# Turning the second memory's score matrices with VectorE and DRAM instead of TensorE

## The chip, the cores and the metric

The kernel runs on one core of a Trainium2 chip. The metric is the device time of one execution in microseconds (us). The kernel before took 2047.61 us, the median of three runs (2044.39, 2047.61 and 2047.65). All profile numbers come from one further execution that the hardware profiler recorded.

## The reference, cut to what matters

The reference is one encoder layer, applied to two independent sequences of 512 tokens by 1024 channels (here called sequence 0 and sequence 1). Each passes through a half-step SwiGLU feed-forward, a mixing block, a second half-step feed-forward and a final RMS norm. The mixing block projects the normed input once and runs two branches side by side: grouped-query attention with 8 heads, and an mLSTM matrix memory with 4 heads of 128 channels that reads in both directions. Each branch is projected back to 1024 channels, gated, summed, and sent through one output projection.

For one memory head the kernel computes, without the reference's chunks,

```
scores[t, s]  = q[t] . k[s] / sqrt(128)                       512 x 512
T[t, s]       = scores * (forward decay weights)  / (forward divisor of t)     for s <= t
              + scores * (backward decay weights) / (backward divisor of t)    for s >= t
h[:, t]       = sum over s of  v[s, :] * T[t, s]                128 x 512
out[:, t]     = sigmoid(o) * head_norm * h[:, t] / rms(h[:, t])
```

T comes out with the query token t on the partitions. The product with v needs the key token s on the partitions, so T has to be turned, once per head and sequence: 512 x 512 float32 values.

## The kernel before, in words

Almost all the work is matmuls on TensorE (PE), each value split into a high and a low part and each product made of three matmuls of 128x128 by 128x512. The feed-forwards stand before and after the mixing; the change touches only the mixing of sequence 1.

`mix(s, ...)` (L841) writes the mixing of sequence s. The weight-bound projections are **units**, pairs of a load and a computation. `go` (L771) issues a unit's weight load, holds the unit, and writes the computation of the oldest held unit once more than `ahead` units are held; for sequence 1 `ahead` is 2 (L844). `queue` and `fill(n)` (L847) feed units to `go`. In sequence 1 all the input projection's weights come back, already split, from DRAM, two DMAs of 512 KB a unit on SyncE's (SP's) queue (L293) into a pool `w8` of 4 buffers. Units used here:

- `mem_values` (L998): four units of 48 matmuls, the values v of all heads;
- `mem_qk(h, j)` (L1009): q or k of head h, 24 matmuls; sequence 1 keeps each result in a tile of the pool `wr` (4 buffers of 4 KB a partition);
- `att_gate`, `out_gate`, `mem_gate(d)`: gates, 24 matmuls each; `mem_gate` keeps its result in a tile of the pool `t2` (11 buffers) until `merge_mem(d)`;
- `merge_att(d)`, `merge_mem(d)`: the branches' projections back, 12 matmuls each.

`mem_head(h)` (L1231) writes a head's scores (12 matmuls, L1241, into two PSUM banks of the pool `ps`), the decay weights on ScalarE (L1255), their product on VectorE (L1257), and the normalisation (L1268 to L1271). It leaves four tiles `Ts[i][0]` of 128x512, one for each block of 128 query tokens.

`mem_out(h, Ts)` (L1274) turns and uses them. For each key block j, four TensorE transposes of 128x128 against the identity (L1283) fill a PSUM bank of the pool `pt`; ScalarE and VectorE split it into high and low parts (`split`, L715 and L716); three matmuls with v (L1291) add it to the bank `po`. Then come the squares, the column sums through VectorE's 32x32 transpose (L225) and a small matmul (L232), the reciprocal root, its spreading (L258), and the split into `mem` (L1302, L715, L716), which `merge_mem` reads.

The order of the instructions on each engine is made by a planner: it takes instructions by priority, which is the order of writing unless `shifted` moves it, and by when its own cost model holds them ready. `pin` (`keep_in_program_order`) ties an instruction to the written order among the pinned instructions of its engine. In the attention part nearly every matmul is pinned; in the memory part of the kernel before none is. The head loop (L1305) writes `mem_head(h)`, some units, `mem_out(h)`, and the rest of the queue, for h = 0 to 3; after it come the eight `mem_gate` and the eight `merge_mem`.

Of the kernel before, what the change touches and what calls it, by code (L numbers as in the profile page):

```python
# [8 lines left out]
F32 = mybir.dt.float32  # L9
F32R = mybir.dt.float32r  # L10
I32 = mybir.dt.int32
AF = mybir.ActivationFunctionType
# [4 lines left out]
P = 128  # L17
S = 512
D = 1024
KD = D // P  # L20
# [6 lines left out]
def encoder(ctx, tc, I, outs):  # L27
    nc = tc.nc
    cpool = ctx.enter_context(tc.tile_pool(name="cpool", bufs=1))
    dpool = ctx.enter_context(tc.tile_pool(name="dpool", bufs=1, space=bass.MemoryType.DRAM))  # L30
    apool = ctx.enter_context(tc.tile_pool(name="apool", bufs=7))
    wpool = ctx.enter_context(tc.tile_pool(name="wpool", bufs=3))
# [9 lines left out]
    def nm(s):  # L42
        n_id[0] += 1
        return f"{s}_{n_id[0]}"
# [241 lines left out]
    def load_w(view, key, park=True):  # L286


        if key in parked:
            d, shape = parked[key]  # L290
            w2 = wpool.tile(shape, F32R, tag="w8", bufs=4, name=nm("w"))
            for i in range(2):
                nc.sync.dma_start(f(w2[:, i]), d[:, i])  # L293
            return w2[:, 0], w2[:, 1]
        raw = fetch_w(view)
        with shifted(-WEIGHTS):
            hi, lo = split_w(raw, V_)
        if not park:
            return hi, lo
        shape = [P, 2] + list(raw.shape[1:])  # L300
        parked[key] = d, _ = dpool.tile(shape, F32, name=nm("wpark")), shape
        for i, t in enumerate((hi, lo)):
            nc.sync.dma_start(d[:, i], f(t))
        return hi, lo
# [3 lines left out]
    V_ = nc.vector  # L308
# [404 lines left out]
    def split(src, hi, lo, eng=None):  # L713

        nc.scalar.activation(hi, src, AF.Copy)  # L715
        (eng or V_).tensor_tensor(lo, src, f(hi), op=ALU.subtract)  # L716
# [3 lines left out]
    HM, DM = 4, 128  # L720
# [46 lines left out]

    held = []
    ahead = [1]

    def go(*units):  # L771
        for load, comp in units:
            held.append((comp, load()))
            while len(held) > ahead[0]:
                c, w = held.pop(0)
                c(w)
# [6 lines left out]
    def tok_proj(xh, xl, cols, kk, done, banks):  # L783

        N = sum(n for _, n in cols)
        p = []

        def load(k0):
            return load_w([win_v[:, k0:k0 + kk, c:c + n] for c, n in cols], ("in", cols[0], k0))

        def comp(k0, w):
            wh, wl = w
            if not p:
                p.extend(b() for b in banks)
            for kl in range(kk):
                k = k0 + kl
                for b in range(4):
                    bs = slice(b * P, (b + 1) * P)
                    for i, (a, w_) in enumerate(((xh, wh), (xh, wl), (xl, wh))):
                        nc.tensor.matmul(p[b][:, :N], a[:, k, bs], w_[:, kl, :],  # L800
                                         start=(k == 0 and i == 0), stop=(k == KD - 1 and i == 2))
# [26 lines left out]
    def proj_w(wh, wl, src, n, p=None):  # L828
        p = p or MM()
        for k in range(n):  # L830
            sh, sl = src(k)
            for i, (a, b) in enumerate(((wh, sh), (wh, sl), (wl, sh))):
                nc.tensor.matmul(p, a[:, k, :], b, start=(k == 0 and i == 0), stop=(k == n - 1 and i == 2))  # L833
        return p

    OUT = 3
    FILLER = 5,3
    SOON = 7,1
    FIRST = 7,9,9,11

    def mix(s, xh, xl, early=None, extra=None, after=None):  # L841

# [8 lines left out]
        def F2(dtype=F32):  # L851
            return T2(dtype, "f2")
# [156 lines left out]
        def mem_qk(h, j):  # L1009
            def done(pp):  # L1010
                if j == 0 and not s:
                    t = wpool.tile([P, 4, S], F32R, tag="w8", bufs=4, name=nm("qk"))
                    qks[h] = [t[:, i] for i in range(4)]
                elif s:
                    t = wpool.tile([P, 2, S], F32R, tag="wr", bufs=4, name=nm("qk"))
                    qks.setdefault(h, []).extend(t[:, i] for i in range(2))
                t = pp
                if not s:
                    t = F2()
                    V_.tensor_tensor(t, pp, R[s], op=ALU.mult)  # L1020
# [135 lines left out]
        for b in range(4):  # L1156
            Ps.append(score(0, b))
            next(rope, None)
            among(FIRST[b])
        last = None  # L1160
        for h in range(HA):
            nxt = []
            for b in range(4):
# [16 lines left out]
                last = h, b, pp  # L1180
# [48 lines left out]
        mem = A([P, HM, 2, S], F32R, "mem")  # L1229

        def mem_head(h):  # L1231
# [39 lines left out]
                    V_.tensor_scalar(tf[:, up_], tb[:, up_], rb, None, op0=ALU.mult)  # L1271
            return Ts

        def mem_out(h, Ts):  # L1274
            vm = Vm[0]
            po = PO()
            hs_ = slice(h * P, (h + 1) * P)
            turned = []
            for j in range(4 + 1):
                if j < 4:  # L1280
                    p = PT()
                    for i in range(4):
                        nc.tensor.transpose(p[:, i * P:(i + 1) * P], Ts[i][0][:, j * P:(j + 1) * P], ident)  # L1283
                    ph, pl = T2(F32R), T2(F32R)
                    split(p, ph, pl)
                    turned.append((j, ph, pl))
                if j >= 1:
                    t, ph, pl = turned.pop(0)
                    with shifted(15):
                        for n, (a, b) in enumerate(((0, ph), (1, ph), (0, pl))):  # L1290
                            nc.tensor.matmul(po, vm[:, a, t, hs_], b, start=(t == 0 and n == 0),  # L1291
                                             stop=(t == 3 and n == 2))
            h2 = T2()
            nc.scalar.activation(h2, po, AF.Square)
            og = ogs[h]
# [9 lines left out]
        for h in range(HM):  # L1305
# [12 lines left out]
            fill(99)  # L1318

        mh, ml = A([P, KD, S], F32R, "mh"), A([P, KD, S], F32R, "ml")  # L1320
        go(*[mem_gate(d) for d in range(KD)])
        go(*[merge_mem(d) for d in range(KD)])
        flush()
        yield None
# [20 lines left out]
    pin = tc.keep_in_program_order  # L1345

    def busy(n, idle):

        for _ in range(n):
# [3 lines left out]
    x2buf = [dpool.tile([P, KD, S], F32, name=f"x2buf{s}") for s in range(2)]  # L1353
    rbuf = [[[dpool.tile([P, 2, S], F32, name=f"rbuf{n}_{j}_{m}") for m in range(7)] for j in range(NF // 2)]
            for n in range(2)]
    xnbuf = dpool.tile([P, KD, S], F32, name="xnbuf")
    raws = [A([P, 4, D], F32, "raw")]
    x0r_ = A([P, KD, S], F32, "x0r")
# [288 lines left out]
    r = [None, None]  # L1647
# [213 lines left out]
```

## Time and profile before

| what | value |
|---|---|
| median of three runs | 2047.61 us (2044.39 to 2047.65) |
| the profiled execution: its own time | 2046.24 us |
| the profiled execution: span from first to last instruction | 2044.5 us |
| TensorE busy | 2034.3 us, 9313 matmuls and transposes |
| VectorE busy | 1571.5 us |
| ScalarE busy | 909.1 us |
| GpSimd busy | 93.6 us |
| granted TensorE clock | 0.999 |
| memory part of sequence 1 in the span, scores of head 0 to output of head 3 | 1180.75 to 1287.4 us |

In the rows below an engine is PE (TensorE matmul), PEld (its weight load), DVE (VectorE), ACT (ScalarE), POOL (GpSimd) or SP (SyncE); a "q" behind it means its sequencer, which issues DMAs. L and a number is a line of the kernel. `out<-in` gives the tiles, `x12` a count. A matmul's record runs to its modelled end, and the next one starts before that, so the distance between two starts, and not the length of a record, is what a matmul costs.

### The profile page before, as it was taken

The numbers are of one execution on the slowest core, as the hardware profiler recorded it, in microseconds if no ns is written. First come the engines' busy times: TensorE is split into PE (matmuls) and PEld (weight loads), VectorE is DVE, ScalarE is ACT, GpSimd is POOL, SyncE is SP. The second block draws the span as 40 slices with busy tenths as digits, with TensorE's granted clock in tenths as the row PEclk, the third lists the DMA queues.
The fourth block names the chain that finished last, engine by engine and source line by source line (L and its number), as shares of the span: only waits on it lengthen the run. The fifth ranks groups of instructions, "written<-read, shape, count | busy, mean of one in ns | idle before, by whom it ended". The sixth has DMA issues, their size and how long they took to land.

```text
span 2044.5 us, 26753 instructions
## 1 busy us (share of the span) xinstructions
PE 2034.3 (100%) x9313; PEld 1680.7 (82%) x9313; DVE 1571.5 (77%) x2780; ACT 909.1 (44%) x1655; POOL 93.6 (5%) x116
## 2 busy tenths in 40 slices
PE   9999999999999999999999999999999999999998
PEld 7888888888888888888888888888888888888887
DVE  7988888886797798786567756366788988786797
ACT  7644444443234577563325554144444444442224
POOL 0000000001003000100120000001000000000001
PEclk9999999999999999999999999999999999999999
DMA  9656566799766853868564345667655655699753
GB/s 308 199 172 224 172 213 187 236 338 362 270 215 223 293 173 130 284 211 292 188 195 139 114 152 169 226 202 225 192 190 181 207 170 180 203 347 341 275 198 119
DMA packets 314727, 445.38 MB, mean 218 GB/s; under 512 B 19848, under 2 KB 189920, under 8 KB 313312
## 3 DMA queue, kind: packets, MB, share of 16 engines
q1 hardware_dynamic: 312512, 437.69, 63.8%
q0 software_dynamic: 1920, 5.72, 0.9%
q8 instruction: 73, 1.20, 0.2%
q14 instruction: 62, 0.51, 0.1%
q10 hardware_dynamic: 160, 0.27, 0.0%
HBM read 284.06 MB, written 159.55 MB: 217 GB/s over the span
## 4 chain that ended last, share of the span: by engine, by line
PE 96%; DVE 2%; ACT 1%; DMA 1%; issue 0%; SPq 0%; DVEq 0%; ACTq 0%
PE mm L833 15%; PE pst L374 12%; PE pso L374 12%; PE mm L374 10%; PE mm L632 8%; PE pss L374 6%; PE mm L820 5%; PE pst L632 4%; PE pss L632 4%; PE mm L800 4%; PE pso L632 3%; PE pso L1121 1%; PE pss L1094 1%; PE pst L1110 1%; PE pso L1291 1%; PE pss L1241 1%
## 5 line engine op out<-in xcount | busy, mean ns | idle before, releaser
L374 PE MATMUL pst<-xc,w 128*128 128x512 f32 x1056 | 253.7, 389 | 0.0
L374 PEld LDWEIGHTS pst<-xc,w 128*128 128x128 f32 x1056 | 198.2, 188 | 41.2
L374 PE MATMUL mm<-xc,w 128*128 128x512 f32 x972 | 229.7, 390 | 0.4 <-ACT f L382 0.4
L374 PEld LDWEIGHTS mm<-xc,w 128*128 128x128 f32 x972 | 182.0, 188 | 38.4 <-ACT f L382 0.8
L632 PE MATMUL mm<-rt,w 128*128 128x512 f32 x765 | 178.7, 389 | 0.0
L833 PE MATMUL mm<-xh,w 128*128 128x512 f32 x560 | 176.9, 392 | 0.0
L632 PEld LDWEIGHTS mm<-rt,w 128*128 128x128 f32 x765 | 143.5, 188 | 29.8
L332 ACT ACTIVATE w<-t 128x512 fp32r<-128x512 f32 x176 | 106.6, 627 | 135.6 <-issue 63.1
L333 DVE TENSOR_TENSOR w<-t,w 128x512 fp32r<-128x512 f32 x176 | 117.8, 687 | 42.9 <-ACT w L332 41.2
L374 PE MATMUL pss<-xc,w 128*128 128x512 f32 x528 | 126.8, 389 | 0.0
L374 PE MATMUL pso<-xc,w 128*128 128x512 f32 x528 | 126.8, 389 | 0.0
L374 PE MATMUL pso<-xc,f 128*128 128x512 f32 x528 | 126.8, 389 | 0.0
L833 PEld LDWEIGHTS mm<-xh,w 128*128 128x128 f32 x560 | 104.9, 188 | 21.9
L374 PEld LDWEIGHTS pss<-xc,w 128*128 128x128 f32 x528 | 99.1, 188 | 20.6
L374 PEld LDWEIGHTS pso<-xc,w 128*128 128x128 f32 x528 | 99.1, 188 | 20.6
L374 PEld LDWEIGHTS pso<-xc,f 128*128 128x128 f32 x528 | 99.1, 188 | 20.6
L820 PE MATMUL mm<-xh,w 128*128 128x512 f32 x336 | 113.4, 400 | 0.0
L833 PE MATMUL mm<-xl,w 128*128 128x512 f32 x280 | 109.6, 391 | 0.0
L715 ACT ACTIVATE w<-wr 128x512 fp32r<-128x512 f32 x72 | 45.1, 632 | 136.7 <-PE pso L632 71.2
L278 ACT ACTIVATE w<-wr 128x1024 fp32r<-128x1024 f32 (+1 forms) x64 | 65.3, 1029 | 79.1 <-issue 23.7
L279 DVE TENSOR_TENSOR w<-wr,w 128x1024 fp32r<-128x1024 f32 (+1 forms) x64 | 79.7, 1247 | 26.5 <-ACT w L278 15.7
L715 ACT ACTIVATE w<-t 128x512 fp32r<-128x512 f32 x82 | 51.8, 632 | 107.6 <-PE pst L632 62.5
(444 smaller groups left out, 4068.7 us busy)
## 6 DMA issues: line engine op xcount, KB each, us to landing
rt<-rbuf SPq DMA_DIRECT2D x154, 512.0 KB, 5.5
wpark<-w SPq DMA_DIRECT2D x88, 512.0 KB, 3.8
w<-wpark SPq DMA_DIRECT2D x88, 512.0 KB, 4.4
wr<-in_ffn_w_gate_dram SPq DMA_DIRECT2D x62, 512.0 KB, 5.3
rbuf<-tab SPq DMA_DIRECT2D x102, 256.0 KB, 4.0
wr<-in_ffn_w_up_dram SPq DMA_DIRECT2D x44, 512.0 KB, 4.5
rbuf<-f SPq DMA_DIRECT2D x72, 256.0 KB, 4.0
wr<-in_w_in_dram SPq DMA_DIRECT2D x36, 512.0 KB, 5.7
```

What stands on the lines that cost most here:

```text
L278: pin(nc.scalar.activation(hi, raw, AF.Copy))
L279: pin(lo_eng.tensor_tensor(lo, raw, f(hi), op=ALU.subtract))
L332: pin(nc.scalar.activation(t[:, 0], src, AF.Copy))
L333: pin(V_.tensor_tensor(t[:, 1], src, f(t[:, 0]), op=ALU.subtract))
L374: nc.tensor.matmul(p, a[:, k, :], xt[:, b, k, :], start=(first and k == 0 and i == 0), stop=(k == HK_ - 1 and i == 2), skip_group_check=True)
L632: nc.tensor.matmul(p, u[:, a, d * P:(d + 1) * P], r[:, b, ts], start=(first and q == 0 and k == 0), stop=(q == len(us) - 1 and k == 2), sk ...
L715: nc.scalar.activation(hi, src, AF.Copy)
L800: nc.tensor.matmul(p[b][:, :N], a[:, k, bs], w_[:, kl, :], start=(k == 0 and i == 0), stop=(k == KD - 1 and i == 2))
L820: pin(nc.tensor.matmul(p[0], a[:, k, :], b, start=(k == 0 and i == 0), stop=(k == n - 1 and i == 2)))
L833: nc.tensor.matmul(p, a[:, k, :], b, start=(k == 0 and i == 0), stop=(k == n - 1 and i == 2))
L1094: pin(nc.tensor.matmul(p, qT[:, h, b * P:(b + 1) * P], kv[:, hk * 2 + j, :], start=(j == 0), stop=(j == 1)))
L1110: pin(nc.tensor.transpose(p[:, b * P:(b + 1) * P], Ps[b][:, kb * P:(kb + 1) * P], ident))
```

## The change

For sequence 1 only:

- `mem_blocks(h, Ts)` is new. VectorE transposes each half row block (128x256) of the four T tiles in 32x32 blocks into two tiles of the pool `wr`: eight instructions a head. Eight DMAs on SP's queue, of 32 partitions each in runs of 512 bytes, put the blocks where they belong in a DRAM buffer; there are two such buffers of 1 MB, used by turns.
- `mem_out` then reads each key block back as a 128x512 tile of the pool `f2` (four DMAs of 256 KB a head, on GpSimd's queue), and splits it from SBUF. No TensorE transposes are left there. The query columns come back in the order (block within 128, block of 128, column), so the output bank `po` has its columns in that order, too; one ScalarE copy a head puts them back into a tile of `t2`, which the squares and the gate read in place of PSUM.
- The head loop is replaced by one written order of heads, units and outputs. `mem_out(h)` is written after `mem_head(h + 1)` and several units. Six `mem_gate` units (`EARLY`) are loaded, and four of them computed, ahead of `mem_out(3)`.
- While this stretch is written, the last matmul of each unit and every matmul of `mem_out` with v is pinned; the score matmuls of `mem_head` aren't.
- q and k of head 2 lie in the tile `mem`, in the places of heads 2 and 3, instead of in `wr`.

The number of units and of their matmuls stays. The core of the diff:

```diff
+    marks = [False]
+    def mark(i, last):
+        return pin(i) if last and marks[0] else i
...
+    EARLY = 6
...
-                    t = wpool.tile([P, 2, S], F32R, tag="wr", bufs=4, name=nm("qk"))
+                    t = mem[:, 2 + j] if h == 2 else wpool.tile([P, 2, S], F32R, tag="wr", bufs=4, name=nm("qk"))
...
+        def mem_blocks(h, Ts):
+
+            q = [wpool.tile([P, 8, 4, 32], F32, tag="wr", bufs=4, name=nm("qt")) for _ in range(2)]
+            for i in range(4):
+                for g in range(2):
+                    V_.transpose(q[g][:, :, i, :],
+                                 Ts[i][0][:, g * 256:(g + 1) * 256].rearrange("p (n m) -> p n m", m=32))
+            for g in range(2):
+                for a in range(4):
+                    nc.sync.dma_start(tbuf[h % 2][8 * g:8 * g + 8, :, a, :].rearrange("n r x -> r n x"),
+                                      q[g][32 * a:32 * a + 32].rearrange("r n i m -> r n (i m)"))
+            return h % 2
...
-                if j < 4:
+                if j < 4 and moved:
+                    p = F2()
+                    nc.gpsimd.dma_start(p, tbuf[Ts][4 * j:4 * j + 4].rearrange("c r a x -> (c r) (a x)"))
+                elif j < 4:
                     p = PT()
                     for i in range(4):
                         nc.tensor.transpose(p[:, i * P:(i + 1) * P], Ts[i][0][:, j * P:(j + 1) * P], ident)
+                if j < 4:
                     ph, pl = T2(F32R), T2(F32R)
                     split(p, ph, pl)
...
+            if moved:
+                rows_ = T2()
+                nc.scalar.activation(rows_.rearrange("p (i a m) -> p i a m", i=4, a=4),
+                                     po.rearrange("p (a i m) -> p i a m", i=4, a=4), AF.Copy)
+                po = rows_
...
+        if s:
+            qk2, qk3 = [[mem_qk(h, j) for j in range(2)] for h in (2, 3)]
+            ma = [merge_att(d) for d in range(KD)]
+            marks[0] = True
+            at = [mem_blocks(0, mem_head(0))]
+            go(*mem_values(), *qk2)
+            at.append(mem_blocks(1, mem_head(1)))
+            go(*qk3, ma[0], ma[1])
+            mem_out(0, at[0])
+            at.append(mem_blocks(2, mem_head(2)))
+            go(att_gate(6), att_gate(7), ma[2], ma[3])
+            mem_out(1, at[1])
+            at.append(mem_blocks(3, mem_head(3)))
+            go(*ma[4:])
+            mem_out(2, at[2])
+            go(*[mem_gate(d) for d in range(EARLY)])
+            mem_out(3, at[3])
+            marks[0] = False
+        for h in range(HM if not s else 0):
...
-        go(*[mem_gate(d) for d in range(KD)])
+        go(*[mem_gate(d) for d in range(EARLY * s, KD)])
...
+    tbuf = [dpool.tile([16, 32, 4, P], F32, name=f"tbuf{i}") for i in range(2)]
```

More of the change, by code (lines that the diff above doesn't have):

```diff
@@ L799, in comp @@
                     for i, (a, w_) in enumerate(((xh, wh), (xh, wl), (xl, wh))):
-                        nc.tensor.matmul(p[b][:, :N], a[:, k, bs], w_[:, kl, :],
-                                         start=(k == 0 and i == 0), stop=(k == KD - 1 and i == 2))
+                        mark(nc.tensor.matmul(p[b][:, :N], a[:, k, bs], w_[:, kl, :],
+                                              start=(k == 0 and i == 0), stop=(k == KD - 1 and i == 2)),
+                             (kl, b, i) == (kk - 1, 3, 2))
             if k0 + kk == KD:
@@ L832, in proj_w @@
             for i, (a, b) in enumerate(((wh, sh), (wh, sl), (wl, sh))):
-                nc.tensor.matmul(p, a[:, k, :], b, start=(k == 0 and i == 0), stop=(k == n - 1 and i == 2))
+                last = k == n - 1 and i == 2
+                mark(nc.tensor.matmul(p, a[:, k, :], b, start=(k == 0 and i == 0), stop=last), last)
         return p
@@ L1272, in mem_head @@
             return Ts
+        def mem_blocks(h, Ts):
[9 more added lines that the diff above has]
+            return h % 2
         def mem_out(h, Ts):
+            moved = isinstance(Ts, int)
             vm = Vm[0]
@@ L1290, in mem_out @@
                         for n, (a, b) in enumerate(((0, ph), (1, ph), (0, pl))):
-                            nc.tensor.matmul(po, vm[:, a, t, hs_], b, start=(t == 0 and n == 0),
-                                             stop=(t == 3 and n == 2))
+                            mark(nc.tensor.matmul(po, vm[:, a, t, hs_], b, start=(t == 0 and n == 0),
+                                                  stop=(t == 3 and n == 2)), True)
             h2 = T2()
+            og = ogs[h]
+            if moved:
[3 more added lines that the diff above has]
+                po = rows_
             nc.scalar.activation(h2, po, AF.Square)
-            og = ogs[h]
             V_.scalar_tensor_tensor(og, og, 1.0, po, op0=ALU.add, op1=ALU.mult)
@@ L1303, in mem_out @@
                 split(og, mem[:, h, 0, :], mem[:, h, 1, :])
-        for h in range(HM):
+        if s:
[17 more added lines that the diff above has]
+        for h in range(HM if not s else 0):
             Ts = mem_head(h)
```

## The prediction

> **What bounds the kernel now.** I read the page's totals and its chain of waits first, then stretches side by side, then TensorE's own timeline.
>
> ```profile
> span 2044.5 us, 26753 instructions
> PE 2034.3 (100%) x9313; PEld 1680.7 (82%) x9313; DVE 1571.5 (77%) x2780; ACT 909.1 (44%) x1655; POOL 93.6 (5%) x116
> GB/s 308 199 172 224 172 213 187 236 338 362 270 215 223 293 173 130 284 211 292 188 195 139 114 152 169 226 202 225 192 190 181 207 170 180 203 347 341 275 198 119
> PE 96%; DVE 2%; ACT 1%; DMA 1%; issue 0%; SPq 0%; DVEq 0%; ACTq 0%
> ```
>
> TensorE is busy for all but 10 us, and 96% of the chain lies on it. A busy TensorE could still hide stretched matmuls, so the next view compares a feed-forward stretch with the stretch of the change: length, then busy time and count per engine, then the granted clock, DMA share and GB/s.
>
> ```profile
> 1600.00:1700.00 100.00, 100.00 (x443) 82.81 (x442) 86.28 (x136) 43.50 (x74) 0.00 (x0) 1.00 0.58 190
> 1200.00:1290.00 90.00, 89.94 (x427) 73.31 (x426) 57.71 (x169) 41.88 (x105) 0.00 (x0) 1.00 0.54 172
> ```
>
> The feed-forward runs 443 matmuls in 100 us, 0.2257 us each. The second stretch holds 64 transposes among its 427, so 363 x 0.2257 = 81.9 us are matmuls at full rate; the other 8.1 us hold the transposes and every bubble. VectorE and ScalarE have slack (58 and 42 of 90 us), GpSimd does nothing there. What is taken off TensorE's list shortens the span, as long as nothing new makes TensorE wait.
>
> **What the removed transposes cost.** The timeline of TensorE in the output of head 1:
>
> ```profile
> 1234.88 0.39 PE L833 MATMUL mm<-xl,w 128*128 128x512 f32 x1
> 1235.11 0.60 PE L1283 MATMUL pst<-ident,t 128*128 128x128 f32 x4
> 1235.46 0.48 PE L1291 MATMUL pso<-t,Vm 128*128 128x512 f32 x1
> 1235.78 0.60 PE L1283 MATMUL pst<-ident,t 128*128 128x128 f32 x4
> 1236.13 2.31 PE L1291 MATMUL pso<-t,Vm 128*128 128x512 f32 x9
> ```
>
> Four transposes hold the next matmul off for 1235.46 - 1235.11 = 0.35 us, and that matmul then takes 0.32 us to its successor in place of 0.23, 0.09 more. A group of four costs 0.44 us; 4 heads x 4 key blocks are 16 groups, 7.1 us. Bounds: 16 x 0.35 = 5.6 us, if the slow next matmul stays, and the 8.1 us above, if every bubble goes. I take **-7.1 us**.
>
> ```profile
> L1283 PE MATMUL pst<-ident,t 128*128 128x128 f32 x64 | 9.0, 274 | 0.0
> ```
>
> A record of one transpose lasts 274 ns; 64 of these end to end would be 17.5 us, but they overlap, and even their union is 9.0. [...]
>
> **What is added on VectorE and ScalarE.** Eight 32x32-block transposes of 128x256 a head. Rows of this stretch:
>
> ```profile
> L225 DVE STREAM_TRANSPOSE f<-t 128x512 f32<-128x512 f32 x4 | 2.8, 704 | 0.0
> L1257 DVE SCALAR_TENSOR_TENSOR t<-pss,t 128x512 f32<-128x512 f32 x8 | 5.5, 687 | 1.3 <-ACT t L1255 1.3
> L1257 DVE SCALAR_TENSOR_TENSOR t<-pss,t 128x256 f32<-128x256 f32 x8 | 3.4, 420 | 0.0
> L716 DVE TENSOR_TENSOR t<-pst,t 128x512 fp32r<-128x512 f32 x26 | 17.3, 687 | 7.9 <-ACT t L715 7.9
> L715 ACT ACTIVATE t<-pst 128x512 fp32r<-128x512 f32 x26 | 14.9, 597 | 8.5 <-PE pst L1283 6.1 <-PE pst L1110 2.2
> L1294 ACT ACTIVATE t<-pso 128x512 f32<-128x512 f32 x4 | 2.4, 598 | 6.4 <-PE pso L1291 6.4
> L715 ACT ACTIVATE att<-f 128x512 fp32r<-128x512 f32 x2 | 1.2, 620 | 0.0
> ```
>
> Halving a VectorE instruction from 512 to 256 columns takes off 267 ns (687 to 420), so a transpose of 256 should take 704 - 267 = 437 ns; bounds 352 (half) and 704. I take 0.44, as its overhead is the nearest known: 3.5 us a head, 14 us in all, beside 57.7 busy of 90. The copy that reorders the output is 0.60 us by the row that reads `po` (0.62 by the one from SBUF; a ragged pattern may cost up to twice that): 2.4 us of ScalarE. Splits from SBUF instead of PSUM are 0.02 us longer on ScalarE and the same on VectorE. All of it lies beside TensorE, and costs nothing while the outputs come in time; if that cover were gone, head 3's copy alone would be on the path, 0.6 us.
>
> **What is moved to the queues, and the wait it adds.** Each head writes 1 MB (8 DMAs on SP's queue) and reads 1 MB (4 on GpSimd's). 8 MB more in the 90 us, beside 172 GB/s x 90 us = 15.5 MB, make 261 GB/s; the page's busiest slice moved 362. There is room, though not for all to be in flight at once.
>
> ```profile
> w<-wpark SPq DMA_DIRECT2D x40, 512.0 KB, 4.4
> rbuf<-f SPq DMA_DIRECT2D x72, 256.0 KB, 4.0
> x2buf<-f POOLq DMA_DIRECT2D x16, 256.0 KB, 3.3
> L1334 POOL DMA_DIRECT2D x2buf<-f x16: 540/557/597, 1033.7 to 1401.5; - x16
> 1219.99 0.92 SPq L1064 DMA_DIRECT2D box<-ebuf  x2
> SPq L293 <- PE mm L833: 54.6, 10, 9.2
> ```
>
> SP issues a DMA in 0.46 us and a weight load at its head stands for up to 9.2 us until TensorE frees a weight buffer; the block stores queue behind it. From a head's normalised tiles to its first matmul with v: transposes 3.5, store issues 8 x 0.46 = 3.7, landing 4.0 (up to twice that for runs of 512 bytes), load issue 0.56, landing 3.3 (up to twice that, with 1 MB asked for at once), split 0.60 + 0.69: 16 to 24 us. And from the first score to the last normalised tile:
>
> ```profile
> 1180.75 1.64 PE L1241 MATMUL pss<-qk,qk 128*128 128x512 f32 x6
> 1197.01 0.61 DVE L1269 SCALAR_TENSOR_TENSOR t<-t,dn,t 128x128 f32<-128x128 f32 x2
> 1256.44 0.84 PE L1241 MATMUL pss<-qk,qk 128*128 128x512 f32 x3
> 1264.31 0.35 DVE L1269 SCALAR_TENSOR_TENSOR t<-t,dn,t 128x128 f32<-128x128 f32 x1 [0.26 <-ACT t L1268]
> ```
>
> 16.9 us for head 0, which shares its time with the attention's end, and 8.2 us for head 2. So an output is ready 25 to 41 us after the head's first score. The cover is what the written order puts between a head's scores and its output, with `go` two units late. Head 0: two units held over, four of `mem_values`, scores of head 1, four `mem_qk`: 348 matmuls, 79 us. Head 1: 192, 43 us (four `mem_qk`, output 0, scores 2, two `merge_att`, two `att_gate`). Head 2: 144, 33 us (`merge_att` 0 and 1, two gates, output 1, scores 3, four `merge_att`). Head 3: 180, 41 us. Only head 2 can be short, by 41 - 33 = 8 us, or 17 with SP's longest wait; with the fast end it has 8 us to spare. Heads 1 to 3 no longer run beside attention, so I lean on the 8.2 us row and charge **+0.8 us**, a twentieth of the worst case. After output 3 four `mem_gate` units (96 matmuls, 21.7 us) still precede `merge_mem`, whose chain gains only the copy: nothing.
>
> Score banks, units and matmul counts are the same; pinning unit ends on an engine that never starves costs nothing in itself. With q and k of head 2 in `mem`, the pool `wr` has its buffers free for the blocks by the time they are needed.
>
> **Sum.** -7.1 + 0.8 = -6.3 us. The profiled execution's 2046.24 us (span and 1.7 us around it) gives 2039.9; it stands 1.4 us under the median of the runs, from which it would be 2041.3. I say **2040.5 us**. Its own range, by the bounds: 2046.24 - 8.1 = 2038.1 to 2046.24 - 5.6 + 0.8 = 2041.4, with the runs' spread of 3 us about 2036 to 2043.5.
>
> **Rivals.** What can be told from no change is about 0.2%, 4.1 us: faster is under 2043.5, slower over 2051.7.
>
> *The round trip is longer than head 2's cover, and the gain is mostly spent.* For it: the 41 us against 33, and TensorE takes its instructions in order, so it stands. Against it: the 8 us to spare at the fast end. It decides no change from 4.4 us of stall (2046.2 - 7.1 + 4.4 = 2043.5); all 8 give 2047.1, and their middle, 6, gives 2045.1. [...]
>
> *Weights come late.* This is the one that ends slower. The stores wait on SP's queue for VectorE's transposes, and the weight loads behind them wait, too. Loads are issued three 24-matmul units ahead, 3 x 24 x 0.227 = 16.3 us; minus 0.9 us for issuing two and 4.4 us for landing, 11 us are to spare. A store that stands at the head of the queue longer than 11 us costs TensorE the excess. With head 0's 16.9 us plus 3.5 of transposes, were the first store put there as the scores begin, that would be 9 us; four heads at 4 us make 16, and 2046.2 - 7.1 + 16 = 2055. It decides slower from 11.2 us of stalls in all (7.1 + 4.1). Against it: the loads of the decay rows (L1064) stand in the same queue today, and TensorE shows no wait for weights.
>
> *The transposes were worth their whole length*: 2046.2 - 17.5 = 2028.7, were the starts misread. The stretch has just 8.1 us besides full-rate matmuls, so hardly.
>
> **How the numbers follow.** The forecast 0.60, the short cover 0.25, late weights 0.12, whole length 0.03. The forecast and the last are faster; of the short cover I count 0.01 as faster and the rest as no change: faster 0.64, same 0.24, slower 0.12. The range 2036 to 2047.5 holds the forecast and nearly all of the short cover, and leaves out late weights and the whole length.
>
> **What would show it.** In the changed kernel's profile: no L1283 of sequence 1, 64 fewer TensorE instructions, and TensorE's busy time lower by about 7 us; in the groups, 32 more transposes of 128x256 on VectorE near 437 ns; sixteen loads on GpSimd's queue near 0.56 us of issue. Right if TensorE has still no idle time beyond some 0.8 us in the stretch. The short cover shows as TensorE waiting, at the matmuls with v of head 2, for ScalarE's or VectorE's split and behind it a DMA from the block buffer; late weights show as waits for `w<-wpark`, and long waits of SP for the transposes. I am wrong if TensorE's idle time grows by more than 3 us, or if the stretch shortens by less than 5 us without any.

## The result, and the profile after

The changed kernel takes 2041.0 us, the median of nine runs (2039.86 to 2041.62); the kernel before, beside it on the same chip, 2045.43 us (nine runs, 2044.39 to 2047.65). The ratio is 0.9975, with a 95% interval of 0.9965 to 0.9985: some 4.4 us, by the interval 3 to 7 us, faster. The profiled execution of the changed kernel took 2039.86 us, 6.4 us less than that of before. First the page of the changed kernel: span, busy time of the engines, and the chain of waits by engine.

```profile
span 2038.1 us, 26750 instructions
PE 2026.7 (99%) x9249; PEld 1672.9 (82%) x9249; DVE 1580.7 (78%) x2812; ACT 912.3 (45%) x1659; POOL 101.2 (5%) x132
PE 93%; DVE 3%; ACT 1%; DMA 1%; issue 1%; SPq 0%; POOL 0%; DVEq 0%; ACTq 0%; POOLq 0%
```

TensorE has the 64 instructions less that were taken off it, and 7.6 us less busy time. But its share of the chain fell from 96% to 93%: a little of the time now goes through VectorE and issues. To see where, I compare TensorE's starts at three places that both kernels have: the first score of the memory's head 0, the first matmul of `merge_mem`, and the first of the second feed-forward (`mm<-xc,w`). The timeline of TensorE, before and then after; the first score of before, at 1180.75, stands in the prediction.

```profile
1335.02 1.30 PE L833 MATMUL pss<-mem,w 128*128 128x512 f32 x5
...
1400.34 1.98 PE L374 MATMUL mm<-xc,w 128*128 128x512 f32 x8
```

```profile
1179.34 1.63 PE L1248 MATMUL pss<-qk,qk 128*128 128x512 f32 x6
...
1327.71 2.88 PE L839 MATMUL pss<-mem,w 128*128 128x512 f32 x12
...
1393.98 4.70 PE L374 MATMUL mm<-xc,w 128*128 128x512 f32 x20
```

The first score already starts 1.4 us earlier. That difference arises in the first 440 us, in code that the change doesn't touch (in the runs below the same point moves between 2.3 us earlier and 1.2 later), so it isn't the change's. From the first score to `merge_mem` it is 154.27 us before and 148.37 after, 5.90 less. From `merge_mem` to the feed-forward it is 65.32 before and 66.27 after, 0.95 more. Together the change is worth **4.95 us** in this pair of profiles. The medians' 4.4 agree.

The same two pieces by windows (length, then busy time and count of PE, PEld, DVE, ACT, POOL, then the clock, DMA share, GB/s); the second runs from the first matmul of the output projection (`mh,w`) to the feed-forward. Before:

```profile
1180.70:1335.00 154.30, 154.24 (x715) 126.21 (x714) 78.40 (x225) 58.17 (x144) 0.00 (x0) 1.00 0.57 188
1356.80:1400.30 43.50, 43.50 (x193) 36.01 (x192) 21.96 (x28) 15.33 (x21) 13.95 (x13) 1.00 0.63 196
```

After:

```profile
1179.30:1327.70 148.40, 147.12 (x651) 119.44 (x650) 86.87 (x255) 61.40 (x148) 8.60 (x16) 1.00 0.76 243
1349.50:1394.00 44.50, 44.20 (x194) 35.72 (x193) 22.98 (x29) 15.68 (x21) 13.65 (x13) 1.00 0.65 198
```

TensorE is busy for 7.1 us less in the stretch, but idles 1.28 us there instead of 0.06, and 0.30 us in the output projection, where it had not idled at all. Where it idles is in its timeline, after:

```profile
1277.20 1.07 PE L1316 MATMUL pso<-t,Vm 128*128 128x512 f32 x4
1279.26 0.73 PE L1316 MATMUL pso<-t,Vm 128*128 128x512 f32 x2 [0.99 <-ACT t L715]
...
1353.47 0.63 PE L839 MATMUL mm<-mh,w 128*128 128x512 f32 x2
1354.40 0.50 PE L839 MATMUL mm<-ml,w 128*128 128x512 f32 x1 [0.30 <-DVE ml L716]
```

The first is the output of head 2, its last key block: it waited for ScalarE's split. The second is the start of the output projection, which waited for VectorE's split of the merged result. ScalarE itself waited for the block from DRAM:

```profile
1278.57 0.63 ACT L715 ACTIVATE t<-f 128x512 fp32r<-128x512 f32 x1 [2.67 <-DMA f<-tbuf]
```

So the next view is GpSimd's timeline, which shows when head 2's four loads were issued and what held them (after):

```profile
1256.00 1.15 POOL L1303 DMA_DIRECT2D f<-tbuf  x2 [3.96 <-DMA tbuf<-qt]
1260.05 0.54 POOL L1303 DMA_DIRECT2D f<-tbuf  x1 [2.91 <-DVE row L226]
1273.97 0.54 POOL L1303 DMA_DIRECT2D f<-tbuf  x1 [13.38 <-DVE box L1332]
```

The first two loads waited for the first half of the stores to land, as they must. The last store was issued by 1255.26 and stores land in 2.6 us in the median, so all the blocks were in DRAM by an estimated 1258. The third and fourth waited for VectorE to finish with something else: L226 is the reduction of the turned squares and L1332 the gate's product that reads the spread root, both of head 1's output, and both read a tile of the pool `f2`. That pool has four buffers, and the blocks take their place in it. The fourth load stood 13.4 us for one, was issued at 1273.97, and came 1 us late.

### The profile page after: what moved, and what is told of

It reads as the page before. It is cut to its first block, busy times and chain, and to the rows that moved or that the text cites. A ratio compares the mean times of both kernels' runs of the same rounds, so it can differ in the third digit from the quotient of the medians.

```text
span 2038.1 us, 26750 instructions
## 1 busy us (share of the span) xinstructions
PE 2026.7 (99%) x9249; PEld 1672.9 (82%) x9249; DVE 1580.7 (78%) x2812; ACT 912.3 (45%) x1659; POOL 101.2 (5%) x132
## 4 chain that ended last, share of the span: by engine, by line
PE 93%; DVE 3%; ACT 1%; DMA 1%; issue 1%; SPq 0%; POOL 0%; DVEq 0%; ACTq 0%; POOLq 0%
PE mm L839 13%; PE pso L374 12%; PE pst L374 12%; PE mm L374 10%; PE mm L632 9%; PE pss L374 6%; PE mm L825 5%; PE pss L632 4%; PE pst L632 4%; PE mm L804 4%; PE pso L632 3%; PE pso L1128 1%; PE pss L1101 1%; PE pst L1117 1%; PE pso L804 1%
## 5 line engine op out<-in xcount | busy, mean ns | idle before, releaser
L278 ACT ACTIVATE w<-wr 128x1024 fp32r<-128x1024 f32 (+1 forms) x64 | 65.3, 1029 | 79.5 <-issue 24.5
```

Of the source, the lines that this page charges most:

```text
L278: pin(nc.scalar.activation(hi, raw, AF.Copy))
```

## The experiments

The theory from these views: the way through DRAM is short enough, and what is lost comes from the pool `f2`. The rivals: the way itself is too long for head 2; the gain and the loss come from the new order rather than from the turn; the transposes' price was misread and the agreement is chance. The table gives every run on sequence 1: median, ratio to the kernel before with its interval, and from the profile the three distances (first score to `merge_mem`; output projection to feed-forward; first score to the end).

| kernel | median us | ratio | score to merge | output projection | score to end |
|---|---|---|---|---|---|
| before | 2045.43 | | 154.27 | 43.56 | 863.70 |
| after | 2041.00 | 0.9975 [0.9965, 0.9985] | 148.37 | 44.51 | 858.75 |
| f2 freed | 2037.99 | 0.9963 [0.9951, 0.9976] | 147.58 | 43.55 | 856.95 |
| transposes put back | 2047.95 | 1.0011 [1.0001, 1.0020] | 154.69 | 45.53 | 866.15 |
| new order, turn on TensorE | 2047.59 | 1.0008 [0.9999, 1.0018] | 154.83 | 44.27 | 865.55 |
| turn through DRAM, old order | 2065.81 | 1.0099 [1.0085, 1.0113] | 174.99 | 43.58 | 884.41 |
| turn left out | 2039.47 | 0.9965 [0.9951, 0.9978] | 146.96 | 43.96 | 856.77 |
| loads on SP's queue | 2043.27 | 0.9987 [0.9978, 0.9996] | 151.18 | 44.58 | 861.61 |
| no pins | 2041.96 | 0.9979 [0.9970, 0.9988] | 149.09 | 45.65 | 860.57 |

From the feed-forward to the end all of them take 644.06 to 644.17 us, but for the new order with the turn on TensorE (644.69), so the distances carry tenths of a microsecond where the medians carry whole ones; but each comes from one execution. A ratio is to the kernel before timed beside that run: 2045.43 us for the changed kernel, 2045.64 for the next four rows, and 2045.82 for the last three.

### f2 freed

```diff
-            row = block_sums(h2)
+            row = block_sums(h2, "t2" if moved else "f2")
...
-                Rh = spread_rows(rh, T2(F32, "f2"))
+                Rh = spread_rows(rh, T2(F32, "t2" if moved else "f2"))
```

The column sums' tiles and the spread root of the moved outputs come from the pool `t2`; `f2` is left to the blocks and to the loads of the next stage.

> The changed kernel, but the work tile of the column sums and the spread root of mem_out take buffers of t2 in place of f2, so that f2 holds block tiles only. Theory A (buffers): the changed kernel lost 1.1 us at the matmuls with v of head 2, whose fourth block load waited on GpSimd's queue for an f2 buffer, and 1.0 us where the output projection starts, because VectorE came 1.0 us late out of loads of f<-x2buf that waited for f2 buffers, too. Both go: 2.1 us less than the changed kernel, some 2039 us. Theory B (the prediction's): the loss is the DRAM round trip or stores late on SP's queue; then the time stays within 0.3 us of the changed kernel, and TensorE still waits at the matmuls of head 2.

Measured: 2037.99 us, 3.0 under the changed kernel by the medians, 1.8 by the distances; the first theory's 2.1 lies between. The two windows of this kernel, and GpSimd's timeline for head 2:

```profile
1179.30:1326.80 147.50, 147.09 (x650) 119.33 (x649) 89.19 (x257) 60.90 (x147) 8.54 (x16) 1.00 0.74 245
1348.60:1392.20 43.60, 43.60 (x194) 36.09 (x193) 21.95 (x28) 15.36 (x21) 13.66 (x13) 1.00 0.63 197
```

```profile
1260.40 1.06 POOL L1303 DMA_DIRECT2D f<-tbuf  x2 [34.21 <-DVE t L225]
1262.01 1.06 POOL L1303 DMA_DIRECT2D f<-tbuf  x2 [0.55 <-DVE row L237]
```

All four loads of head 2 are out by 1263, eleven microseconds earlier than the last one was, and the wait at the products with v is gone; the stretch is 0.79 us shorter than in the changed kernel. The output projection is back at 43.6 us without idle time. The second effect runs through SP's queue. There the next stage's loads of the residual (`f<-x2buf`) stand, into `f2` too. SP's timeline, before, after, and with f2 freed:

```profile
1292.34 1.32 SPq L1686 DMA_DIRECT2D f<-x2buf  x3
1303.65 0.37 SPq L1686 DMA_DIRECT2D f<-x2buf  x1
```

```profile
1312.31 1.14 SPq L1735 DMA_DIRECT2D f<-x2buf  x1
1321.22 0.32 SPq L1735 DMA_DIRECT2D f<-x2buf  x1
1325.34 0.91 SPq L1735 DMA_DIRECT2D f<-x2buf  x2
```

```profile
1303.94 1.52 SPq L1735 DMA_DIRECT2D f<-x2buf  x3
1317.12 0.32 SPq L1735 DMA_DIRECT2D f<-x2buf  x1
```

In the changed kernel they are 20 us later than before, and VectorE, which waits for them in its own order, reaches the merge with them still to do (its timeline, before and then after):

```profile
1338.01 0.69 DVE L1222 SCALAR_TENSOR_TENSOR t<-t,pss 128x512 f32<-128x512 f32 x1 [27.02 <-PE pss L833]
```

```profile
1330.40 1.42 DVE L711 SCALAR_TENSOR_TENSOR f<-f,gain,R 128x512 f32<-128x512 f32 x2 [5.51 <-DMA f<-x2buf]
1331.73 0.68 DVE L1229 SCALAR_TENSOR_TENSOR t<-t,pss 128x512 f32<-128x512 f32 x1
```

Before, VectorE had long been waiting for TensorE when the merges began, and started the first one (L1222) 2.99 us after the first `merge_mem` matmul (1338.01 - 1335.02). After, it starts it (L1229) 4.02 us behind that matmul (1331.73 - 1327.71), 1.03 later. From there to the output projection it waits once, 0.70 us for ScalarE, as it does before, and the 1.03 us are about what TensorE loses at 1353 to 1354 (0.95 by the distance). One edit that touches only the pools removes both stalls, so the sharing of `f2` is the cause of both.

### Transposes put back

Four transposes of the identity, into a `pt` bank that nobody reads, at the places of the old ones; the turn through DRAM stays.

```diff
+                if j < 4 and moved:
+                    x_ = PT()
+                    for i in range(4):
+                        mark(nc.tensor.transpose(x_[:, i * P:(i + 1) * P], ident, ident), True)
```

> The changed kernel with 16 groups of four TensorE transposes of the identity put back where the turns were, read by nobody. This is the price of the transposes alone. By the distance of starts: 16 x 0.44 = 7.1 us more than the changed kernel, 2048.1 us. By the length of their records: 64 x 0.274 = 17.5 us more, 2058.5. If TensorE had slack in this stretch: nothing.

Measured: 6.95 us over the changed kernel by the medians, 7.4 by the distances (6.3 in the stretch, 1.0 in the output projection). Window of the stretch, and the group of the added transposes:

```profile
1179.20:1333.90 154.70, 154.30 (x715) 126.09 (x714) 86.73 (x255) 61.45 (x148) 8.59 (x16) 1.00 0.74 233
```

```profile
L1311 PE MATMUL pst<-ident 128*128 128x128 f32 x64 | 8.9, 272 | 0.0
```

In the stretch TensorE is busy for 7.2 us more than in the changed kernel, and idle for 0.9 us less, since the transposes fill most of the wait at head 2. Sixty-four records of 272 ns, 17.4 us end to end, thus cost 7 us, 0.11 us each: the distance between starts, not the record.

### New order, turn on TensorE

The written order, the pins and the place of q and k of head 2 as in the changed kernel, with the old transposes. Since the four tiles of T can't be kept for two heads, each output stands ahead of the next head's scores.

```diff
-            at = [mem_blocks(0, mem_head(0))]
+            t0 = mem_head(0)
             go(*mem_values(), *qk2)
-            at.append(mem_blocks(1, mem_head(1)))
+            mem_out(0, t0)
+            t1 = mem_head(1)
...
```

> The new written order of units with its pinned unit ends, but the turns on TensorE as before, and so mem_out(h) right after the units that follow mem_head(h). Theory: the order gives nothing by itself; the time is that of the kernel before, 2045.4 us, within 1 us. Rival: a good part of the gain is the order and the pins; then 2041 to 2043.

Measured: no gain; 1.95 us more than before by the medians, where within 1 us was said, though the interval still holds no difference. By the distances it is 1.85 us more, 0.56 in the stretch, 0.71 in the output projection, and 0.58 in the second feed-forward, which it doesn't touch. In the stretch TensorE is as busy as before:

```profile
1178.50:1333.30 154.80, 154.59 (x715) 126.43 (x713) 75.20 (x223) 58.05 (x144) 0.00 (x0) 1.00 0.56 180
```

So the gain comes from the turn; this order by itself gains nothing. (It isn't quite the changed kernel's, as each output stands earlier in it.) Here, too, the residual's loads come late (the last at 1331.16), though no block takes an `f2` buffer: the outputs' own `f2` tiles, used up to the new order's later end, may be enough for that, which no run isolates.

### Turn through DRAM, old order

```diff
-        if s:
+        if False:
...
-        for h in range(HM if not s else 0):
-            Ts = mem_head(h)
+        for h in range(HM):
+            Ts = mem_blocks(h, mem_head(h)) if s else mem_head(h)
...
-        go(*[mem_gate(d) for d in range(EARLY * s, KD)])
+        go(*[mem_gate(d) for d in range(KD)])
```

> The turns through VectorE and DRAM in the head loop of before, nothing pinned. Theory: the old loop writes two units (5 to 11 us) between a head's last tile and its output, where the way through DRAM takes 16 to 24 us, so TensorE waits 5 to 18 us a head: 2045 - 7 + 4 x 8 = 2070, at least 2050. Rival: the planner moves other units ahead by itself and the order isn't needed: 2041 to 2043.

Measured: 20 us slower than before, although the transposes are gone. Of the 175.0 us from the first score to `merge_mem` TensorE is idle for 22.4, most of it in one wait (waits of TensorE, total, times, longest); it also works at half its clock for a while behind that wait, as the last section shows:

```profile
PE pso L1316 <- ACT t L715: 19.1, 3, 17.1
```

Heads 0 to 2 the planner covers with what else is at hand, for 2 us; at head 3 nothing is left, and TensorE stands 17.1 us. So the total came near the first theory, but not the wait at every head. That makes this kernel the place to measure the way through DRAM with nothing ahead of it. Its timelines of VectorE, SP, GpSimd, ScalarE and TensorE, one fence each:

```profile
1308.16 0.31 DVE L1276 SCALAR_TENSOR_TENSOR t<-t,dn,t 128x128 f32<-128x128 f32 x1
1308.39 2.40 DVE L1286 STREAM_TRANSPOSE qt<-t 128x256 f32<-128x256 f32 x7
```

```profile
1310.49 3.96 SPq L1290 DMA_DIRECT2D tbuf<-qt  x8
```

```profile
1315.13 1.06 POOL L1303 DMA_DIRECT2D f<-tbuf  x2 [31.49 <-DMA tbuf<-qt]
1317.16 1.06 POOL L1303 DMA_DIRECT2D f<-tbuf  x2 [0.97 <-DMA tbuf<-qt]
```

```profile
1319.54 1.35 ACT L715 ACTIVATE t<-f 128x512 fp32r<-128x512 f32 x2 [11.80 <-DMA f<-tbuf]
```

```profile
1320.22 5.68 PE L1316 MATMUL pso<-t,Vm 128*128 128x512 f32 x12 [17.10 <-ACT t L715]
```

The last normalised tile is done at 1308.47; the first block is split from 1319.54 on, and the first product starts at 1320.22: 11.8 us in all. The steps overlap. The last store is issued by 1314.45, and the second pair of loads, which waits for the stores to land, goes out at 1317.16, 2.7 us later; the first pair has left two microseconds before. This is one head's way, and not a bound: the first load here is split 4.4 us after its issue, while a load's landing takes 6.1 us in the median of the changed kernel.

### Turn left out

`mem_blocks` does nothing, and the outputs split rows of the attention's result, which lie ready in SBUF.

```diff
+            return h % 2
             q = [wpool.tile([P, 8, 4, 32], F32, tag="wr", bufs=4, name=nm("qt")) for _ in range(2)]
...
-                    p = F2()
-                    nc.gpsimd.dma_start(p, tbuf[Ts][4 * j:4 * j + 4].rearrange("c r a x -> (c r) (a x)"))
+                    p = f(att[:, j, 0, :])
```

> The changed kernel with the turns left out: VectorE's block transposes, the stores and the loads are gone, and mem_out splits the rows of the attention's output tile in place of the turned scores, so its result no longer depends on the scores. All else stays. Theory A: the way through DRAM costs TensorE only what e3_f2_free took back; first score to first merge of sequence 1 then lasts 147.0 to 147.6 us as there, and the whole 2037.5 to 2038.3 us. Theory B: the added VectorE work (14 us) or the 8 MB of DMA cost something more; then it comes out more than 1 us under e3_f2_free.

Measured: 856.77 us from the first score to the end, against 856.95 with f2 freed and 858.75 in the changed kernel. The stretch:

```profile
1178.70:1325.60 146.90, 146.48 (x650) 119.74 (x649) 76.37 (x223) 60.77 (x147) 0.00 (x0) 1.00 0.58 189
```

With no transposes on VectorE, no stores and no loads, it saves 7.3 us of the stretch; with f2 freed the whole turn saves 6.7. So by these profiles the way through DRAM, VectorE's transposes included, costs 0.2 us (to the end) to 0.6 us (in the stretch) once its buffers are free. The output projection is 0.4 us longer than before even here, and the residual's loads are late here, too (the last at 1323.45): with 10.5 us less of VectorE's time in the stretch the late loads cost less than in the changed kernel, not nothing. The medians (2039.47 here, 2037.99 there) stand the other way round, and the median here lies outside the first theory's 2037.5 to 2038.3. The profiled execution here (2037.22 us) is the fastest of its four, so the medians bound the price of the way no closer than a microsecond or two.

### Loads on SP's queue

```diff
-                    nc.gpsimd.dma_start(p, tbuf[Ts][4 * j:4 * j + 4].rearrange("c r a x -> (c r) (a x)"))
+                    nc.sync.dma_start(p, tbuf[Ts][4 * j:4 * j + 4].rearrange("c r a x -> (c r) (a x)"))
```

> The changed kernel with the sixteen block loads on SP's queue instead of GpSimd's. In the changed kernel the loads stood on GpSimd's queue for up to 13.4 us until an f2 buffer came free. On SP's queue the same waits hold the weight loads behind them, and these have 11 us to spare. Theory: 2 to 8 us slower than the changed kernel, with TensorE waiting for w<-wpark. Rival: the planner places the loads where their buffer is free, and the time is that of the changed kernel within 1 us.

Measured: 2.3 us over the changed kernel by the medians, 2.9 by the distances. It got slower, but not by weights: no wait of TensorE was for one. Waits in the window from 1260 to 1310 us:

```profile
ACT t L715 <- DMA f<-tbuf: 12.6, 6, 5.7
...
PE mm L839 <- ACT t L873: 1.9, 1, 1.9
```

The loads of head 3 left SP's queue at 1288.90, behind that head's eight stores; ScalarE stood 5.7 us for the first, the gates' activations (L873) behind it in ScalarE's order stood as well, kept their PSUM banks, and TensorE waited 1.9 us for one. GpSimd's queue, which has nothing else to do there, is worth 2 to 3 us.

### No pins

```diff
-            marks[0] = True
+            marks[0] = False
```

> The changed kernel without the pins: neither the unit ends nor the matmuls with v are tied to the written order. Theory: the order of writing sets the priorities and the pins change nothing: within 1 us of the changed kernel. Rival: the planner takes the outputs early by its own times for the way through DRAM, and TensorE waits there: 2 us or more slower.

Measured: 1.0 us over the changed kernel by the medians, 1.8 by the distances (0.7 in the stretch, 1.1 in the output projection). By the medians the theory, within 1 us, holds, and the two ratios' intervals overlap; by the single profile the pins help by 1.8 us. Either way the planner alone nearly finds the order.

### Sequence 0 as well

Three kernels extend the version with f2 freed to sequence 0, whose weights are raw and are split as they come. The edit of the first:

```diff
-        if s:
+        if True:
...
-        for h in range(HM if not s else 0):
+        for h in range(0):
...
-        go(*[mem_gate(d) for d in range(EARLY * s, KD)])
+        go(*[mem_gate(d) for d in range(EARLY, KD)])
```

> e3_f2_free, with the same turns and the same written order for sequence 0 also (its q and k stay in w8, its weights still come raw into wr and are split). Theory: the 64 transposes of sequence 0 are worth as much, so 6 to 7 us less than e3_f2_free's 2038.0: 2031.5 us. Rival: in sequence 0 the blocks take two of the four wr buffers that the raw weights need, or only one unit is held ahead, and TensorE waits for weights: from 2034 up to over 2045.

Measured: 2114.39 us where 2031.5 was said, a ratio of 1.0332 [1.0316, 1.0347], and 74 us more than with f2 freed between the first projection of k and v of sequence 0 and that of sequence 1. Waits of TensorE and then of SP, from 800 to 985 us:

```profile
PE mm L839 <- ACT w L278: 21.3, 5, 6.7
PE pss L1248 <- DVE t L1264: 18.6, 5, 6.4
```

```profile
SPq L1071 <- ACT t L1262: 51.4, 4, 34.0
SPq L1290 <- DVE qt L1286: 42.2, 4, 24.1
SPq L303 <- ACT w L278: 40.8, 8, 10.6
```

TensorE waits for weights that ScalarE has still to split (L278), and for VectorE's products with the scores (L1264), while at the head of SP's queue decay rows (L1071) wait for ScalarE (21.0 us in the kernel before), and the block stores (L1290) for VectorE's transposes. The waits aren't all of the loss. From 790 to 985 us TensorE is idle for 54.6 us, and its granted clock is 0.83, where it is 1.00 with f2 freed: it is busy for 140.4 us with 525 instructions, which at the rate there (921 in 194.9 us) would be an estimated 111 us of work. GpSimd adds the decay rows of sequence 0 in one order with its block loads, which stood for up to 42.1 us; the second kernel gives these rows to VectorE.

```diff
-            (V_ if s or not h else G_).tensor_tensor(em3, eb3, tabs[3][:, d].unsqueeze(1).to_broadcast([P, 4, P]), op=ALU.add)
+            V_.tensor_tensor(em3, eb3, tabs[3][:, d].unsqueeze(1).to_broadcast([P, 4, P]), op=ALU.add)
```

> e11_both, but the decay rows of sequence 0 are added on VectorE, as those of sequence 1 are, in place of GpSimd. In e11_both these additions stood on GpSimd's queue behind block loads that waited up to 42 us for an f2 buffer. Theory C: that queue caused the larger part of the 76 us lost, and the time falls by at least 30 us, to 2080 or less. Theory D: the stores on SP's queue, which waited up to 24 us for VectorE's transposes with the raw weights behind them, caused it; then it falls by less than 15 us.

Measured: 2111.6 us, 1.0324 [1.0308, 1.0339], 3 us less by the medians, with intervals that overlap: GpSimd's order isn't the larger part of the cause. The third also takes the tiles of q and k of sequence 0 from `t2`.

```diff
-                    t = F2()
+                    t = T2()
                     V_.tensor_tensor(t, pp, R[s], op=ALU.mult)
```

> e13_both_rows, and the scaled q and k of sequence 0 pass through t2 in place of f2, so that block loads of sequence 0 wait for f2 buffers less. Theory C: the loads no longer hold anything, and a few us more are gained. Theory D: the raw weights behind the stores still set the time, within 5 us of e13_both_rows. If neither queue is left as a cause, it reaches the 2031.5 us that 64 more transposes would give.

Measured: 2122.29 us, 1.0376 [1.0359, 1.0394], worse by 11 us. The edit does free the loads of head 0, which go out from 829.9 to 833.0 us where in the second kernel they go out from 869.1 to 889.1, and the time doesn't fall: that these came late isn't the cause. Of the later loads some still stand for up to 40.8 us (40.9 there) behind VectorE, and the run leaves their part open. That the raw weights come late behind SP's waits fits the rows above (in all three kernels L1071 waits 50 to 57 us and L1290 41 to 49), but no run isolates it. What it is in sequence 0 stays open.

Not tried: a fifth buffer for `f2` or for `wr`, and the new order with the transposes on TensorE two heads back, in which the tiles of T would never come free.

## Why the prediction was right, and where it was not

**The time.** 2040.5 us was said and 2041.0 measured; faster was said, at 0.64. The time came out closer than the gain, and that is luck. The prediction started from the one execution of 2046.24 us and the median of three, 2047.61; by nine runs the kernel before takes 2045.43, from which its -6.3 us would have given 2039.1. A base that was too high and a gain that was too large cancelled. The sum, -6.3 us, is -4.95 in the profiles' distances and -4.4 by the medians. The difference has a place: the loss of 0.8 was 2.1.

**The removed transposes, -7.1 us.** Right. Putting them back costs 7.0 to 7.4 us, with 7.2 us more of TensorE's busy time in the stretch; leaving the whole turn out saves 7.3 in the stretch, TensorE's busy time there fell by 7.1. The bounds of 5.6 and 8.1 hold. The rival by the whole record (17.5 us) falls with the transposes put back.

**What is added on VectorE and ScalarE, at nothing.** Right in size; the groups of the changed kernel from 1180 to 1290 us:

```profile
L1286 DVE STREAM_TRANSPOSE qt<-t 128x256 f32<-128x256 f32 x32 | 11.4, 409 | 0.0
...
L1303 POOL DMA_DIRECT2D f<-tbuf x16 | 8.6, 539 | 207.7 <-DMA tbuf<-qt 151.3 <-DVE box L1332 30.9 <-DMA w<-wpark 14.5
...
L1322 ACT ACTIVATE t<-pso 128x512 f32<-128x512 f32 x3 | 1.8, 598 | 4.9 <-PE pso L1316 4.9
```

A transpose takes 409 ns where 437 was said, the reordering copy 598 where 0.60 us was: no more than the 598 of L1294 before, which read `po` in order, so nothing shows the allowance of twice that for a ragged pattern. A split from SBUF takes 623 ns on ScalarE and 682 on VectorE, one from PSUM 598 and 692. A load's issue takes 539 where 0.56 us was, and 537 to 544 in all sixteen. Their landing takes 6.1 us in the median from GpSimd's queue and 4.3 from SP's, in the run that moved them there, and no run separates the queue from the other traffic. What made the fourth load of head 2 late was a buffer.

**The stall at head 2, +0.8 us.** The place was right, the products with v of head 2, and so was the sign by which it would show, a wait for ScalarE's split with a DMA behind it. The cause was not. The step "from a head's normalised tiles to its first matmul with v: ... 16 to 24 us" added in sequence what overlaps, and took 4 to 8 us for a store that lands in about 2.7: the way takes 11.8 us at head 3 of the old order. For a load it took 3.3 to 6.6, and the median was 6.1. Its allowances of twice as long, for runs of 512 bytes and for 1 MB at once, came from no row, and no run shows either by itself: the stores, in such runs, landed in 2.6 us in the median, and the loads in 3.1 to 8.0. What failed beside it is the sentence on buffers: it counted those of `wr`, into which the blocks are written, and not those of `f2`, into which they come back. The fourth load stood 13.4 us for one. The stall cost 1.15 us by TensorE's starts (the 0.99 of the row, and the slow matmuls around it). A charge of 0.8 made for another cause came near it by luck.

**After output 3, nothing.** Wrong by 0.95 us. The step "merge_mem, whose chain gains only the copy: nothing" looked at the chain, and not at VectorE's place in it: the residual's loads, which share `f2`, came 20 us late, VectorE entered the merges a microsecond late, and TensorE met that 22 us later, at the output projection.

**The rivals.** The short cover came true in place and kind, at 1.15 us instead of 4.4 to 8, and for another reason. That TensorE stands at such a wait is in the timeline: it idled for 0.99 us ahead of the product with v at 1279.26, though a unit of `merge_att` that was under way at 1276.97 still had a matmul (`mm<-att,w`) to start, at 1279.82. Late weights did not come in sequence 1, where no wait of TensorE in the stretch is for `w<-wpark`; in sequence 0 waits for weights are a part of the 74 us, whose cause is open.

**What was given as wrong-if** (idle time of over 3 us more, or a stretch shorter by less than 5 us without any) did not happen: 1.2 us more of idle time in the stretch, 5.90 us shorter. Its sign of being right was missed, if by little: no idle time beyond some 0.8 us was said, and it is 1.28.

**A better version.** With f2 freed the kernel takes 2037.99 us, 7.65 us under the kernel before (2045.64 beside it) by the medians and 6.75 by the distances; it beats both.

## What to carry to other kernels

When a transfer is put in place of an engine's work, count the buffers that it lands in and who else holds them, not only its length: here the way of 11.8 us was covered, and a load stood 13.4 us for a landing buffer that another step held, while the next stage's loads lost their place in the same pool. Price what is taken off a busy TensorE by the distance between starts around it (0.11 us a transpose here), never by the length of its records (0.27). And a round trip through DRAM needs its cover in the written order: the same turn gained 5 us with work placed between the scores and the products, and lost 20 in the old order.

## What was not expected of the hardware

After TensorE's wait of 17.1 us at head 3 (turn through DRAM, old order) its clock was at half. Windows of that kernel, cut where the granted clock changes; the number behind POOL's busy time is that clock:

```profile
1304.69:1308.10 3.41, 0.00 (x0) 0.00 (x0) 3.34 (x11) 2.44 (x5) 0.00 (x0) 1.00 0.90 309
1308.10:1325.17 17.07, 4.91 (x10) 3.08 (x11) 5.29 (x13) 2.52 (x4) 2.13 (x4) 0.50 0.87 244
1325.17:1328.58 3.41, 1.52 (x6) 0.86 (x5) 2.09 (x4) 2.55 (x5) 0.00 (x0) 1.00 0.43 138
1328.58:1332.00 3.42, 3.42 (x10) 2.74 (x9) 1.89 (x11) 0.13 (x1) 0.00 (x0) 0.50 0.27 77
```

TensorE stopped at 1303.12 and its clock fell 5.0 us later; it started again at 1320.22 and the clock came back 5.0 us after that. In these 5 us ten matmuls start where 22 would at full rate, so this wait cost an estimated 2.7 us beside itself (twelve matmuls of 0.2257 us). Then, after 3.41 us in which TensorE was busy for 1.52, the clock falls again, for 3.42. The wait of 0.99 us in the changed kernel left it at 1.00 (mean from 1276 to 1282 us).

The stretches between these changes last 17.07 (five times 3.41), 3.41 and 3.42 us. Ahead of the first fall lie 3.41 us without a matmul; ahead of the return TensorE was busy for 4.94 of the 5.00 us from 1320.20; ahead of the second fall for 1.52 of 3.41 us. From 1332 to 1337 us, behind the 3.42 us that it filled at half clock, it is at 1.00 again. How long TensorE must idle for the clock to fall, and how much work brings it back, this one case doesn't show.
